# Two 64-row matmuls in the two halves of TensorE's array, in place of two zero-padded 128-row ones, for attention scores and the scan's masked products

## Chip, cores and metric

One core of one Trainium2 chip. The metric is the device time of one launch in microseconds (us), median of several runs. PE is TensorE's matmul, PEld its weight load, DVE VectorE, ACT ScalarE, POOL GpSimd, SP SyncE.

## What is computed

Two layers (`DEPTH`) of a hybrid network over 512 latent tokens and 128 context tokens. Each layer normalises and modulates its input, projects it once, and gives the columns to three mixers: a bidirectional RWKV-7 scan (4 heads of 64 features, width 256), differential attention (4 heads, each with **two maps of 64 features** and 128 value features), and a Hyena long convolution. Their outputs go through one output projection and then a squared-ReLU MLP. The two parts that matter here, from the reference:

```
s = jnp.einsum('bqhmd,bkhmd->bhmqk', qblk, k).astype(jnp.float32) * scale     # d = 64, m = 2 maps
p = jax.nn.softmax(s, axis=-1)
wts = p[:, :, 0] - lam * p[:, :, 1]
...
sa = jnp.einsum('bhvk,bhk->bhv', s, -kk_t)                                    # scan, 64 features per head
s = (s * w_t[:, :, None, :] + sa[..., None] * (kk_t * a_t)[:, :, None, :]
     + v_t[..., None] * k_t[:, :, None, :])
```

The kernel computes the scan in chunks of 128 tokens. For a chunk and a head it needs four 128x128 products over 64 features: (B or K) against (Z and R), each masked to its triangle.

## The kernel before

The five token tiles of 128 (four latent, one context) go through a layer in stages: input projection with Hyena and the operands of the scan, attention, scan, output projection, MLP. The instructions are written in Python order, but a scheduler that simulates the program (`schedule_with_timeline_sim=True`, L1772) sets the order on every engine; a pool's buffer that is still read holds an instruction back in that order.

**Attention** (L610 to L731) treats units of one head and one token tile: 4 heads x 5 tiles x 2 layers = 40 units. Three stages of successive units are issued interleaved.

- `at_head` (L637) loads a head's keys `kr` and queries. The queries stand in `qp` twice, a plane for each map, with the other map's 64 rows set to zero by two memsets on POOL (L645, L646), so that a product over 128 rows gives one map's scores. The rotated queries are written by two DVE additions of 64 rows each (L659).
- `at_scores` (L671): for each of two maps, scores of 128 queries against 640 keys (512 and 128 columns, L682 and L683; a context tile has 128 columns alone, L685) into a PSUM tile `pss` of two banks; the minimum (DVE, L687); the exponential with its sum (ACT, L689). Then DVE combines the two maps (L698). There are two `pss` buffers: map 0 takes one, map 1 the other.
- `at_values` (L701) transposes the weights (`pst`, L170) and multiplies by the values (`pso`, L714); `at_out` normalises and transposes back (`psy`).

**Scan** (`rw_begin`, `rw_scan`, `rw_inverse`, `rw_states`): 40 chunks (2 layers, 2 head pairs, 2 directions, 5 tiles), two by two in 20 groups. `rw_inverse` (L1001) first makes the masked products of each chunk. ACT copies B and K into a zeroed tile `bp`, one head's 64 rows at a time (L1019, L1020), the other head's rows staying zero; then for q = B, K and for each head e a 128-row matmul of 256 columns (L1025) into a PSUM bank `b` for each q, and a DVE product with the mask for each bank (L1026), giving `gb` and `gk`. POOL makes the fp16 matrix `m` from `gb` (L1032). Six doublings follow on PE (L1053, L1058, L1060), each with DVE and ACT steps between. `rw_states` then carries the states. Groups, states of both directions and the next modulation's products (`psmod`, L293) are woven together. The first four chunks' products are issued during the last units of attention.

Of the kernel before, what the change touches and what calls it, by code (L numbers as in the profile page):

```python
# [9 lines left out]
F32 = mybir.dt.float32  # L10
# [3 lines left out]
ALU = mybir.AluOpType  # L14
# [16 lines left out]
# columns of the small-vector table  # L31
# [15 lines left out]
def _consts():  # L47
    """Arrays that depend on the shapes alone."""
# [63 lines left out]
class Net:  # L112
# [26 lines left out]
    def split(self, h, l, src, he="v", le="v"):  # L139
        """h + l = src exactly to 24 bits, each of 12 bits."""  # L140
# [31 lines left out]
    def mm3(self, out, a, b, first, last):  # L172
        """out += a[0..1]^T b[0..1] over the split parts"""
# [23 lines left out]
    def setup(self):  # L197
# [15 lines left out]
        # conditioning: silu(c), silu(c_ctx) as columns padded to 32  # L213
# [24 lines left out]
    def small(self, l):  # L238
        """small vectors of layer l"""
# [12 lines left out]
        nlam = self.t(pl, [P, 1], F32, "nlam")       # -lambda  # L252
# [8 lines left out]
        hb = self.t(pl, [P, 8], F32, "hb")           # halves of w0, a0  # L261
# [48 lines left out]
    def mod_cols(self, rows):  # L310
        """the rows as columns: (q, 32 j + c), of which c < 2 used"""
# [20 lines left out]
    def mod_rows(self, rows, js):  # L332
        """gate * g_post of latents and context, into DRAM"""
# [5 lines left out]
    def mod_gate(self, d, pool):  # L339
        """the same on every partition"""  # L340
# [30 lines left out]
    def rstd(self, pool, ss, n, eps, shape, nm="rstd"):  # L371
        """(ss / n + eps) ** -0.5"""
# [32 lines left out]
    def denseB(self, pss, srcs, act, order=None, need=None):  # L405
        """token-major: 512 columns into 5 PSUM tiles [128, 512]; srcs: per pair of k tiles [128, 2, 512]"""
# [19 lines left out]
    def dense_apart(self, ws, act):  # L426
        """the same, one token tile after the other, with weights loaded before: yields (tile, PSUM)"""
# [8 lines left out]
    def ff_load(self, sa, px):  # L436
        """the weight side of a pair, in split parts: B11 B21, then T1 B22, T2 T3, T4"""
# [36 lines left out]
    def ff_plain(self, sa, sb, px, A, tmp, f):  # L474
        """two column tiles in eight products"""
# [41 lines left out]
    def ff_first(self, ys):  # L517
        """the blocks of the first half of the tokens"""
# [8 lines left out]
    def ff_rest(self, ys, A, pool, tmp):  # L527
        """the others: first those that plain products need"""
# [60 lines left out]
    def headscale(self, pool, sq, n, eps, fn):  # L589
        """sq: feature-major tile; (sum over a head / n + eps) ** -0.5, per head, back on its features: fn(slice, PSUM)"""  # L590
# [19 lines left out]
    def attention(self, l, pool, head, fill):  # L610
        """the stages of successive (head, token tile) units are issued interleaved"""
# [25 lines left out]
    def at_head(self, l, h):  # L637
        """q and k of a head, with their positions; k: latents, cache, context"""
# [5 lines left out]
        qp = self.at_tile("qp")  # L644
        nc.gpsimd.memset(qp[64:, 0], 0.0)  # L645
        nc.gpsimd.memset(qp[:64, 1], 0.0)  # L646
        for m in range(2):
            r = slice(64 * m, 64 * m + 64)
            nc.sync.dma_start(qp[r, m, TL:], self.Qd[h][r, TL:])
        for isq in range(2):  # L650
# [5 lines left out]
            if isq:  # L656
                for m in range(2):
                    r = slice(64 * m, 64 * m + 64)
                    nc.vector.tensor_tensor(out=qp[r, m, :TL], in0=u[r], in1=sh[r], op=ALU.add)  # L659
            else:  # L660
                nc.vector.tensor_tensor(out=kr[:, :TL], in0=u, in1=sh, op=ALU.add)
# [9 lines left out]
    def at_scores(self, u, pool):  # L671
        """both maps' exponentials (the products come with the factor -1/8), and their difference (times the first map's sum)"""
# [1103 lines left out]
```

## Time and profile before

| | |
|---|---|
| runs of the kernel before | 2267.98, 2269.1, 2275.34 us, median 2269.1 |
| the profiled execution: span, first to last instruction | 2272.8 us |
| mean granted TensorE clock | 0.968 |
| busy share PE, PEld, DVE, ACT, POOL | 94%, 80%, 64%, 36%, 35% |

The profiled execution's own device time is listed in no other form than its span, which lies 3.7 us (0.16%) above the median of the runs. Differences below are worked out on the span's rows and applied to the median.

Stages by the first and last instruction of their lines, in us from the span's start: attention 389 to 471 and 1474 to 1573 (the first part of the second lies beside the last products of the stage ahead), scan 471 to 700 and 1573 to 1762.

How to read it: a matmul of two fp32 operands is two instructions (passes) in the trace, so the 160 products of L1025 stand as x320. A record's duration has the pipeline's depth in it; the time that a matmul takes of PE is the distance between successive starts. The shapes show rows x columns of the weights (`64*128` is a matmul over 64 rows).

### The profile page before, as it was taken

The page shows a single profiled execution, that of the slowest core. Times are in us where ns is not written, and L with a number is a line of the kernel's source. Part 1 is how long each engine was busy: PE and PEld are TensorE (multiplying, and loading weights), DVE is VectorE, ACT ScalarE, POOL GpSimd, SP SyncE. Part 2 cuts the span into 40 slices and gives each one's busy share as a digit, 9 for nine tenths or more (in the row PEclk, how much of TensorE's full clock was granted, in tenths as well). Part 3 has the DMA queues.
Part 4 walks back from the last instruction along what each step waited for, and adds up shares of the span by engine and source line. Part 5 has one row for each costly group of instructions (what it writes and reads, how often), then busy time and mean ns, then how long its engine had stood idle before and what let it go on. Part 6 is the DMA issues. An engine that isn't in the chain of part 4 may idle for free.

```text
span 2272.8 us, 34001 instructions
## 1 busy us (share of the span) xinstructions
PE 2141.8 (94%) x13236; PEld 1815.5 (80%) x13236; DVE 1453.2 (64%) x2188; ACT 825.1 (36%) x1644; POOL 802.4 (35%) x781
## 2 busy tenths in 40 slices
PE   7999998899999899999999999989999989999998
PEld 2799985566687799898988999756588878989896
DVE  6776657865575764655666575886576484647475
ACT  4542232553342533222324323355344352313131
POOL 3433433641112424351522343363112232524251
PEclk8899998999999899999999999999999999999999
DMA  8244432135405222222244343222510512222233
GB/s 303 78 140 157 131 99 67 54 114 197 169 3 182 75 84 76 86 72 93 74 168 173 105 121 101 80 70 96 197 46 23 201 53 84 84 75 84 84 100 123
DMA packets 86070, 245.42 MB, mean 108 GB/s; under 512 B 12195, under 2 KB 24995, under 8 KB 85908
## 3 DMA queue, kind: packets, MB, share of 16 engines
q1 hardware_dynamic: 80148, 222.34, 28.8%
q0 software_dynamic: 5760, 20.91, 3.0%
q8 instruction: 104, 1.70, 0.3%
q14 instruction: 58, 0.48, 0.1%
HBM read 214.80 MB, written 28.87 MB: 107 GB/s over the span
## 4 chain that ended last, share of the span: by engine, by line
PE 43%; DVE 6%; issue 3%; POOL 3%; ACT 2%; DMA 2%; DVEq 0%; SPq 0%; POOLq 0%; ACTq 0%
PE psB L176 5%; PE psB L177 5%; PE psA L388 5%; PE psB L175 5%; PE psF L177 3%; PE psF L176 3%; PE psF L175 3%; PE b L1025 1%; PE psmod L293 1%; PE pss L682 1%; DMA ffb<-in_w_ff_dram 1%; PE pso L714 1%; PE psD L177 1%; PE psD L176 1%; PE psD L175 1%
## 5 line engine op out<-in xcount | busy, mean ns | idle before, releaser
L388 PE MATMUL psA<-act,wh 128*128 128x320 f32 x1472 | 305.6, 321 | 1.2 <-ACT uhr L1503 0.5
L388 PEld LDWEIGHTS psA<-act,wh 128*128 128x128 f32 x1472 | 241.0, 194 | 10.7 <-issue 8.0
L177 PE MATMUL psB<-wh,f 128*128 128x512 f32 x560 | 218.1, 389 | 0.0
L176 PE MATMUL psB<-wl,f 128*128 128x512 f32 x560 | 218.0, 389 | 0.0
L143 POOL TENSOR_TENSOR wl<-wr,wh 128x1024 fp32r<-128x1024 f32 x42 | 105.2, 2505 | 308.5 <-DVE wh L149 140.6
L175 PE MATMUL psB<-wh,f 128*128 128x512 f32 x560 | 209.1, 389 | 0.0
L388 PE MATMUL psA<-act,wl 128*128 128x320 f32 x736 | 183.0, 319 | 0.8 <-DVE wl L143 0.8
L143 DVE TENSOR_TENSOR wl<-wr,wh 128x1024 fp32r<-128x1024 f32 x84 | 106.6, 1269 | 64.4 <-ACT wh L147 62.8
L457 POOL TENSOR_TENSOR fft<-ffb 128x512 f32<-128x512 f32 x56 | 90.9, 1623 | 127.2 <-DVE wl L143 53.8
L388 PEld LDWEIGHTS psA<-act,wl 128*128 128x128 f32 x736 | 128.8, 194 | 4.6 <-issue 3.1
L147 ACT CAST wh<-wr 128x1024 fp32r<-128x1024 f32 x63 | 66.1, 1050 | 168.4 <-PE psB L177 82.5
L177 PEld LDWEIGHTS psB<-wh,f 128*128 128x128 f32 x560 | 105.1, 188 | 21.9
L175 PEld LDWEIGHTS psB<-wh,f 128*128 128x128 f32 x560 | 105.1, 188 | 21.7
L176 PEld LDWEIGHTS psB<-wl,f 128*128 128x128 f32 x560 | 105.1, 188 | 21.6
L149 DVE CAST wh<-wr 128x1024 fp32r<-128x1024 f32 x63 | 49.9, 793 | 93.5 <-PE psB L177 64.8
L1054 DVE TENSOR_TENSOR x<-b,cmask 128x512 f16<-128x512 f32 x120 | 80.4, 685 | 33.0 <-PE b L1053 32.7
L147 ACT CAST f<-ffr 128x640 fp32r<-128x640 f32 x64 | 43.8, 726 | 154.1 <-DVE ffr L497 154.1
L1063 ACT CAST t<-px 128x512 f16<-128x512 f32 x100 | 58.7, 588 | 101.4 <-PE px L1058 100.3
L505 DVE TENSOR_TENSOR ffr<-ffr,psF 128x320 f32<-128x320 f32 x140 | 67.3, 481 | 37.3 <-POOL ffr L505 20.3
L505 POOL TENSOR_TENSOR ffr<-ffr 128x320 f32<-128x320 f32 x56 | 55.3, 987 | 94.6 <-DVE ffr L505 86.6
L1025 PE MATMUL b<-ZR,bp 128*128 128x256 f32 x320 | 85.4, 392 | 1.5 <-ACT awt L147 0.7
L177 PE MATMUL psF<-ffS,wl 128*128 128x320 f32 x256 | 80.3, 314 | 5.0 <-DVE wl L143 5.0
(461 smaller groups left out, 6041.7 us busy)
## 6 DMA issues: line engine op xcount, KB each, us to landing
wr<-in_w_mod_dram SPq DMA_DIRECT2D x83, 512.0 KB
wr<-in_w_ff_dram SPq DMA_DIRECT2D x72, 512.0 KB
wr<-in_w_in_dram SPq DMA_DIRECT2D x46, 512.0 KB
x<-x SPq DMA_DIRECT2D x30, 512.0 KB
ffa<-in_w_ff_dram SPq DMA_DIRECT2D x28, 512.0 KB
ffb<-in_w_ff_dram SPq DMA_DIRECT2D x28, 512.0 KB
dft<-in_k_dftf_dram POOLq DMA_DIRECT2D x16, 512.0 KB, 7.2
dft<-in_k_dfti_dram POOLq DMA_DIRECT2D x16, 512.0 KB, 4.7
```

Source lines behind the costliest of these rows:

```text
L143: eng.tensor_tensor(out=l, in0=src, in1=h.bitcast(F32), op=ALU.subtract)
L147: self.nc.scalar.copy(out, in_)
L149: self.nc.vector.tensor_copy(out, in_)
L175: nc.tensor.matmul(out, a[0], b[0], start=first, stop=False)
L176: nc.tensor.matmul(out, a[0], b[1], start=False, stop=False)
L177: nc.tensor.matmul(out, a[1], b[0], start=False, stop=last)
L388: self.nc.tensor.matmul(ps[:, hf, :320], (h, l)[a][:, k * P:(k + 1) * P], act[b][k][:, hf * 320:hf * 320 + 320], start=k == 0 and i == 0, ...
L457: sub = lambda o, x, y: nc.gpsimd.tensor_tensor(out=o, in0=x, in1=y, op=ALU.subtract)
L505: add = lambda o, a, b, e=nc.vector, op=ALU.add: e.tensor_tensor(out=o, in0=a, in1=b, op=op)
L1025: nc.tensor.matmul(ps[:, 2 * e:2 * e + 2], bp[:, q, e], s["ZR"][:, :, j], start=True, stop=True)
L1054: nc.vector.tensor_tensor(out=vw(x16), in0=vw(ps), in1=cm(i), op=ALU.mult)
L1063: nc.scalar.copy(t16, ps1)
```

## The change

`at_head` no longer makes two padded planes: `qp` is one plane, both maps' features stacked on 128 rows, one load and one DVE addition, no memset. `at_scores` takes both `pss` buffers at once and multiplies rows 0 to 63 for map 0 and rows 64 to 127 for map 1, written in turn. In the scan the `bp` tiles, their memsets and the ACT copies go; each head's product reads its 64 rows of `BK` and `ZR` directly. The products are now stored by chunk (`gt[i]`, with q, head and mask inside) instead of by q, and a PSUM bank now belongs to a head e instead of to q. POOL's operation for `m16` becomes two, one per chunk.

```
 # at_head
-        qp = self.at_tile("qp")
-        nc.gpsimd.memset(qp[64:, 0], 0.0)
-        nc.gpsimd.memset(qp[:64, 1], 0.0)
-        for m in range(2):
-            r = slice(64 * m, 64 * m + 64)
-            nc.sync.dma_start(qp[r, m, TL:], self.Qd[h][r, TL:])
+        qp = self.at_tile("qp")[:, 0]
+        nc.sync.dma_start(qp[:, TL:], self.Qd[h][:, TL:])
...
-            if isq:
-                for m in range(2):
-                    r = slice(64 * m, 64 * m + 64)
-                    nc.vector.tensor_tensor(out=qp[r, m, :TL], in0=u[r], in1=sh[r], op=ALU.add)
-            else:
-                nc.vector.tensor_tensor(out=kr[:, :TL], in0=u, in1=sh, op=ALU.add)
+            nc.vector.tensor_tensor(out=(qp if isq else kr)[:, :TL], in0=u, in1=sh, op=ALU.add)
 # at_scores
+        pss = [self.t(self.pss, [P, 1024], F32, "pss") for _ in range(2)]
+        for a, b, o in ((0, TL, 0), (TL, T, TL)) if lat else ((T, T + TC, 0),):
+            for m in range(2):
+                r = slice(64 * m, 64 * m + 64)
+                nc.tensor.matmul(pss[m][:, o:o + b - a], H["qp"][r, j * P:(j + 1) * P], H["kr"][r, a:b],
+                                 start=True, stop=True)
         for m in range(2):
-            q = H["qp"][:, m, j * P:(j + 1) * P]
-            ps = self.t(self.pss, [P, 1024], F32, "pss")
-            if lat:
-                nc.tensor.matmul(ps[:, :TL], q, H["kr"][:, :TL], start=True, stop=True)
-                nc.tensor.matmul(ps[:, TL:T], q, H["kr"][:, TL:T], start=True, stop=True)
-            else:
-                nc.tensor.matmul(ps[:, :TC], q, H["kr"][:, T:T + TC], start=True, stop=True)
+            ps = pss[m]
 # rw_inverse
-            bp = self.bp[self.nbp % 2]          # (B | K) by head, the other head's rows zero
-            self.nbp += 1
-            nc.scalar.copy(bp[:64, :, 0], s["BK"][:64, :, j])
-            nc.scalar.copy(bp[64:, :, 1], s["BK"][64:, :, j])
-            gm = self.gmask[:, s["d"]].rearrange("p (a t) -> p a t", a=2).unsqueeze(1).to_broadcast([P, 2, 2, P])
-            for q, g in ((0, gb), (1, gk)):
-                ps = self.bank4(self.b1, "b1")
+            gm = self.gmask[:, s["d"]].unsqueeze(1).to_broadcast([P, 2, 2 * P])
+            ps = [self.bank4(self.b1, "b1") for _ in range(2)]
+            for q in range(2):
                 for e in range(2):
-                    nc.tensor.matmul(ps[:, 2 * e:2 * e + 2], bp[:, q, e], s["ZR"][:, :, j], start=True, stop=True)
-                nc.vector.tensor_tensor(out=g[:, i].rearrange("p e a t -> p e (a t)"),
-                                        in0=ps.rearrange("p (e a) t -> p e (a t)", e=2),
-                                        in1=gm.rearrange("p e a t -> p e (a t)"), op=ALU.mult)
+                    hs = slice(64 * e, 64 * e + 64)
+                    nc.tensor.matmul(ps[e][:, 2 * q:2 * q + 2], s["BK"][hs, q, j], s["ZR"][hs, :, j],
+                                     start=True, stop=True)
+            for e in range(2):
+                nc.vector.tensor_tensor(out=gt[i][:, :, e].rearrange("p q a t -> p q (a t)"),
+                                        in0=ps[e].rearrange("p (q a) t -> p q (a t)", q=2), in1=gm, op=ALU.mult)
             yield
```

The scheduler orders the changed program anew. Two places, both on PE, show how.

First place: PE, attention of the first layer, second head, token tiles 1 and 2. `pss_927` and `pss_930` (before), `pss_927` and `pss_928` (now) are the two maps of tile 1; `pst`, `psy` and `pso` are transposes and value products of other units. Before:

```order
L682 MATMUL pss_927_4067<-kr_839_3847,qp_840_3850 128x512
L683 MATMUL pss_927_4067<-kr_839_3847,qp_840_3850 128x128
L170 MATMUL pst_918_4048<-ident_25_130,pexp_888_3977 128x128
L682 MATMUL pss_930_4074<-kr_839_3847,qp_840_3850 128x512
L683 MATMUL pss_930_4074<-kr_839_3847,qp_840_3850 128x128
L714 MATMUL pso_919_4051<-vt_812_3781,awt_917_4047 128x128
L682 MATMUL pss_953_4142<-kr_839_3847,qp_840_3850 128x512
L683 MATMUL pss_953_4142<-kr_839_3847,qp_840_3850 128x128
```

Now:

```order
L674 MATMUL pss_927_4059<-kr_839_3843,qp_840_3846 128x512
L674 MATMUL pss_927_4059<-kr_839_3843,qp_840_3846 128x128
L170 MATMUL psy_904_4010<-ident_25_130,aon_900_4002 128x128
L674 MATMUL pss_928_4060<-kr_839_3843,qp_840_3846 128x512
L674 MATMUL pss_928_4060<-kr_839_3843,qp_840_3846 128x128
L706 MATMUL pso_919_4043<-vt_812_3777,awt_917_4039 128x128
L674 MATMUL pss_953_4130<-kr_839_3843,qp_840_3846 128x512
L674 MATMUL pss_953_4130<-kr_839_3843,qp_840_3846 128x128
```

Map 0's two matmuls still come first and map 1's two behind them, with a 128-row transpose between; what the program text writes in turn does not stand in turn.

Second place: PE, the end of the first layer's attention, where the first scan chunk's products come in. `b1_1164` and `b1_1165` (before) are the banks of B and K, `b1_1162` and `b1_1163` (now) those of the two heads. Before:

```order
L682 MATMUL pss_1167_4677<-kr_1053_4389,qp_1054_4392 128x512
L683 MATMUL pss_1167_4677<-kr_1053_4389,qp_1054_4392 128x128
L714 MATMUL pso_1153_4640<-vt_1119_4563,awt_1150_4630 128x128 x4
L1025 MATMUL b1_1164_4668<-ZR_677_2884,bp0_1160_4660 128x256 x2
L714 MATMUL pso_1153_4640<-vt_1119_4563,awt_1150_4630 128x128
L1025 MATMUL b1_1165_4672<-ZR_677_2884,bp0_1160_4660 128x256 x2
L682 MATMUL pss_1170_4684<-kr_1053_4389,qp_1054_4392 128x512
```

Now:

```order
L674 MATMUL pss_1165_4655<-kr_1053_4377,qp_1054_4380 128x512
L674 MATMUL pss_1165_4655<-kr_1053_4377,qp_1054_4380 128x128
L706 MATMUL pso_1153_4624<-vt_1119_4547,awt_1150_4614 128x128 x4
L1012 MATMUL b1_1162_4646<-ZR_677_2884,BK_681_2900 128x256 x2
L706 MATMUL pso_1153_4624<-vt_1119_4547,awt_1150_4614 128x128
L1012 MATMUL b1_1163_4647<-ZR_677_2884,BK_681_2900 128x256 x2
L674 MATMUL pss_1166_4656<-kr_1053_4377,qp_1054_4380 128x512
```

Head 0's two products (q = B, K) stand together, then a 128-row value product, then head 1's two: in place of one switch of bank there is now one of array rows.

## Rows read from the trace of the kernel before

**Rows 1.** Busy time of the engines in six stretches, attention (two per layer) and scan; columns first.

```profile
core 0: us, PE busy (x) PEld busy (x) DVE busy (x) ACT busy (x) POOL busy (x), PEclk, DMA share, GB/s
388.00:430.00 42.00, 31.50 (x142) 21.74 (x141) 36.04 (x68) 20.44 (x62) 26.06 (x36) 0.89 0.32 99
430.00:471.00 41.00, 38.50 (x224) 28.08 (x223) 30.17 (x63) 28.08 (x96) 20.86 (x44) 0.99 0.10 32
471.00:700.00 229.00, 220.95 (x1859) 159.69 (x1858) 140.25 (x271) 93.69 (x212) 45.36 (x55) 0.99 0.40 131
1478.00:1530.00 52.00, 42.18 (x211) 29.09 (x210) 44.45 (x90) 28.40 (x93) 33.73 (x54) 0.90 0.21 64
1530.00:1573.00 43.00, 38.94 (x228) 29.36 (x227) 30.53 (x58) 27.44 (x92) 19.92 (x40) 1.00 0.11 38
1573.00:1762.00 189.00, 183.26 (x1680) 139.06 (x1679) 120.06 (x237) 81.04 (x175) 39.44 (x41) 1.00 0.31 103
```

**Rows 2.** Chain that ended last, by line, in the second layer's scan (1573 to 1762).

```profile
by line: PE b L1025 15.3%; PE psmod L293 15.0%; PE px L1058 7.3%; PE px L1060 6.8%; PE b L1053 6.8%; PE px L1073 5.7%; PE pq L1099 4.7%; PE px L1068 4.3%; PE pq L1093 4.0%; PE pq L1129 3.4%; PE pq L1104 2.4%; PE pq L1090 2.4%; PE pq L1105 2
```

**Rows 3.** The same in the second layer's attention (1478 to 1573).

```profile
by line: PE pss L682 22.4%; PE pso L714 14.8%; ACT pexp L689 7.9%; issue 5.9%; PE pss L683 5.1%; PE pst L170 5.1%; PE b L1025 4.1%; DVE amin L687 3.5%; DVE pexp L698 2.9%; DVE acf L694 2.6%; DVE ql L655 2.4%; POOL aon L728 2.4%; ACT awt L14
```

**Rows 4.** What PE waited for longest, in the second layer's scan.

```profile
PE ps L917 <- DVE yacc L1132: 1.6, 1, 1.6
```

**Rows 5.** The same in the second layer's attention.

```profile
PE pss L682 <- ACT pexp L689: 5.4, 7, 2.6
```

**Rows 6.** PE around a 64-row product in the stage of the scan's operands: start, length, line, count.

```profile
1392.73 0.60 PE L388 MATMUL psA<-act,wh 128*128 128x320 f32 x3
1393.17 0.38 PE L170 MATMUL pshb<-ident,ksq 128*128 128x128 f32 x2
1393.48 1.34 PE L585 MATMUL ps<-u,w 64*128 64x320 f32 x4
1393.85 0.70 PE L585 MATMUL ps<-u,w 64*128 64x320 f32 x2
1394.12 0.70 PE L585 MATMUL ps<-u,w 64*128 64x320 f32 x2
1394.75 0.56 PE L388 MATMUL psA<-act,wl 128*128 128x320 f32 x2
1395.15 0.31 PE L388 MATMUL psA<-act,wh 128*128 128x320 f32 x1
```

**Rows 7.** PE at products in separate column groups: modulation (32 columns), then outputs (64 columns).

```profile
1617.16 1.91 PE L293 MATMUL psmod<-wr,sc 128*32 128x512 f32 x12
1619.00 0.40 PE L1058 MATMUL px<-x,tt 128*128 128x128 f16 x4
...
1710.51 0.45 PE L1129 MATMUL pq<-gk,vt 128*64 128x128 f32 x4
1710.78 0.40 PE L1130 MATMUL pq<-gb,sA 128*64 128x128 f32 x4
1711.11 0.48 PE L1025 MATMUL b<-ZR,bp 128*128 128x256 f32 x1
```

**Rows 8.** ACT and PE in attention: the sums that end two exponentials, then the next unit's scores.

```profile
1489.62 0.20 ACT L689 ACTIVATION_READ_ACCUMULATOR pexp<-pss,amin 128x1 f32 x1
...
1489.87 1.13 PE L682 MATMUL pss<-kr,qp 128*128 128x512 f32 x2 [1.14 <-ACT pexp L689]
...
1490.39 0.21 ACT L689 ACTIVATION_READ_ACCUMULATOR pexp<-pss,amin 128x1 f32 x1
...
1491.06 1.28 PE L714 MATMUL pso<-vt,awt 128*128 128x128 f32 x10
```

**Rows 9.** Groups of instructions by line and shape that the change removes or halves.

```profile
L1025 PE MATMUL b<-ZR,bp 128*128 128x256 f32 x320 | 85.4, 392 | 1.5 <-ACT awt L147 0.7 <-DVE x L1054 0.6
L1019 ACT COPY bp<-BK 64x256 f32<-64x256 f32 x40 | 16.0, 401 | 24.2 <-PE b L1025 19.1 <-POOL bp L845 4.9
L659 DVE TENSOR_TENSOR qp<-ql,rsh 64x512 f32<-64x512 f32 x16 | 10.9, 683 | 0.1
```

More of the change, by code (lines that the diff above doesn't have):

```diff
@@ L842, in rw_begin @@
         nc = self.nc
-        self.bp = [self.t(pool, [P, 2, 2, P], F32, f"bp{i}", bufs=1) for i in range(2)]
-        for x in self.bp:
-            nc.gpsimd.memset(x, 0.0)
-        self.nbp = self.ng = 0
+        self.ng = 0
         def groups(p):
@@ L1013, in rw_inverse @@
         self.ng += 1
-        gb, gk = (x.rearrange("p (i e a t) -> p i e a t", i=2, e=2, a=2) for x in (gb, gk))
-        G["gb"], G["gk"] = gb, gk
+        gt = [x.rearrange("p (q e a t) -> p q e a t", q=2, e=2, a=2) for x in (gb, gk)]
+        G["g"] = gt
         for i, (s, j) in enumerate(ent):
-            bp = self.bp[self.nbp % 2]
-            self.nbp += 1
-            nc.scalar.copy(bp[:64, :, 0], s["BK"][:64, :, j])
-            nc.scalar.copy(bp[64:, :, 1], s["BK"][64:, :, j])
-            gm = self.gmask[:, s["d"]].rearrange("p (a t) -> p a t", a=2).unsqueeze(1).to_broadcast([P, 2, 2, P])
-            for q, g in ((0, gb), (1, gk)):
-                ps = self.bank4(self.b1, "b1")
-                for e in range(2):
-                    nc.tensor.matmul(ps[:, 2 * e:2 * e + 2], bp[:, q, e], s["ZR"][:, :, j], start=True, stop=True)
-                nc.vector.tensor_tensor(out=g[:, i].rearrange("p e a t -> p e (a t)"),
-                                        in0=ps.rearrange("p (e a) t -> p e (a t)", e=2),
-                                        in1=gm.rearrange("p e a t -> p e (a t)"), op=ALU.mult)
+            gm = self.gmask[:, s["d"]].unsqueeze(1).to_broadcast([P, 2, 2 * P])
+            ps = [self.bank4(self.b1, "b1") for _ in range(2)]
+            for q in range(2):
+                for e in range(2):
+                    hs = slice(64 * e, 64 * e + 64)
[4 more added lines that the diff above has]
+                                        in0=ps[e].rearrange("p (q a) t -> p q (a t)", q=2), in1=gm, op=ALU.mult)
             yield
@@ L1031, in rw_inverse @@
         m16 = H("m16", 5)
-        nc.gpsimd.tensor_tensor(out=m16.rearrange("p (i e) t -> p i e t", i=2), in0=gb[:, :, :, 0],
-                                in1=self.ident.unsqueeze(1).unsqueeze(1).to_broadcast([P, 2, 2, P]), op=ALU.add)
+        for i in range(2):
+            nc.gpsimd.tensor_tensor(out=m16[:, 2 * i:2 * i + 2], in0=gt[i][:, 0, :, 0],
+                                    in1=self.ident.unsqueeze(1).to_broadcast([P, 2, P]), op=ALU.add)
         if mixed:
@@ L1067, in rw_inverse @@
         for u in us:
-            nc.tensor.matmul(ps[:, u], gb[:, u // 2, u % 2, 0], t16[:, u], start=True, stop=True)
+            nc.tensor.matmul(ps[:, u], gt[u // 2][:, 0, u % 2, 0], t16[:, u], start=True, stop=True)
         nc.vector.tensor_tensor(out=t16, in0=ps, in1=t16, op=ALU.subtract)
@@ L1080, in rw_states @@
         nc, O = self.nc, self.O
-        gb, gk, tf = G["gb"], G["gk"], G["tf"]
+        gt, tf = G["g"], G["tf"]
         for i in idx:
@@ L1092, in rw_states @@
                 es = slice(64 * e, 64 * e + 64)
-                nc.tensor.matmul(px[:, es], gk[:, i, e, 0], vt[:, j, es], start=not lat, stop=e == 1 or not lat)
+                nc.tensor.matmul(px[:, es], gt[i][:, 1, e, 0], vt[:, j, es], start=not lat, stop=e == 1 or not lat)
             X = self.t(pool, [P, P], F32, "sX")
@@ L1128, in rw_states @@
                 es = slice(64 * e, 64 * e + 64)
-                nc.tensor.matmul(py[es], vt[:, j, es], gk[:, i, e, 1], start=not lat, stop=False)
-                nc.tensor.matmul(py[es], SA[:, es], gb[:, i, e, 1], start=False, stop=True)
+                nc.tensor.matmul(py[es], vt[:, j, es], gt[i][:, 1, e, 1], start=not lat, stop=False)
+                nc.tensor.matmul(py[es], SA[:, es], gt[i][:, 0, e, 1], start=False, stop=True)
             if j in done:
```

## Prediction

> **What bounds the kernel now.** I read the stages first, because the change touches only attention and scan. The stretches [rows 1] show two kinds of stage. In the scan PE is busy 221 of 229 us and 183 of 189 us, at a clock of 0.99 and 1.00, while ACT and DVE stand at 41% to 64%; in the first half of each attention PE has 31.5 of 42 us and 42.2 of 52 us, and DVE more than PE (36.0 and 44.5 us); in the second half PE leads again (38.5 of 41, 38.9 of 43). The chain of the second scan [rows 2] is PE nearly throughout, L1025 and the modulation first with 15% each. The chain of attention [rows 3] is mixed: scores 22% and 5%, value products 15%, but exponentials, minima, combinations and POOL between them. The waits agree: in the scan PE's longest is 1.6 us [rows 4], in attention it waits seven times, 5.4 us, for an exponential to free a score buffer [rows 5]. So in the scan each microsecond on PE is a microsecond of time; in attention about half of one is.
>
> **What a matmul costs.** Successive passes of 320 fp32 columns start 0.27 us apart (1393.85, 1394.12 [rows 6]), so 128 columns take 0.107, 256 take 0.21, 512 take 0.43. These are the passes of a 64-row product: half the rows alone makes nothing shorter. The gain can only come from two halves running beside each other.
>
> Do parts of the array run beside each other? The trace has it for column groups: twelve modulation passes of 512 columns take from 1617.16 to 1619.00, 1.84 us, where one after the other would be 12 x 0.43 = 5.1; eight passes of L1129 and L1130 take from 1710.51 to 1711.11, 0.60 us with the return to the whole array in it, where singly they are 0.86 [rows 7]. The program has L1129 and L1130 of one half ahead of those of the other, so the halves overlap even when four passes stand between. Row halves I take to do the same if nothing else stands between; no row here shows it.
>
> **What a change of shape costs.** The array must go over to the other shape and back. Between the start of L170 at 1393.17 and that of the L388 at 1395.15 lie 1.98 us [rows 6]. The passes in it are 2 x 0.107, 4 x 0.27 and 2 x 0.147 (L388 starts three times in 0.44 us before), 1.58 us. The rest, 0.40, is one way out and one back: **0.20 us per change of shape**, in which neither a matmul streams nor a weight load hides.
>
> The Trainium skill, "TensorEngine Tiling (Array Packing)", gives up to twice the speed for a contraction of at most 64 (section Theoretical Speedup). By that alone, every pair at half its time, the scan's 40 chunks would save 34 us of PE and the 32 latent units 34, half of it on the path: 51 us, 2218. The same page says that changing the tiling mode drains TensorE (section Key Properties), without a price; by the 0.20 us above, the drains as they stand in the new order would take back about as much (250 x 0.20). Which of the two wins hangs on the order, next.
>
> **The change, part by part.**
>
> (1) *Do the halves meet?* The order of PE's instructions decides it, and the two places shown with the change are typical. Counted over the program, the two maps of a latent unit stand together in 14 of 32 units; in 18 something of 128 rows is between. In the scan the two heads of a chunk stand together in 2 of 40 chunks; 76 bursts of two products stand alone. A buffer for the second half comes free later than for the first, and the scheduler fills the time with other work.
>
> (2) *Scan, loss.* Over both scans the order now holds 338 changes of array shape where it held 212 (the modulation's and the outputs' column groups), 126 more: 126 x 0.20 = **+25 us**. (3) *Scan, gain.* Two chunks overlap; a chunk is 8 passes of 0.21, 1.7 us, half of it saved: **-1.7**. PE's short waits there, 1.6 us the longest [rows 4], take back perhaps 4 in both scans. Scan: **+19**.
>
> (4) *Attention, loss.* No change of shape before, 124 now (61 and 63): +25 us of PE. In the first halves of the stage PE has 10 us per layer without any record [rows 1], and many bursts begin after a wait, where the array is empty anyway. (5) *Attention, gain.* A latent map is 2 x 0.43 + 2 x 0.107 = 1.07 us, which is the most that a pair can save. But map 1's buffer is not free when map 0 starts: at 1489.87 map 0 starts as the exponential of the unit before ends (1489.62 + 0.20), and the other exponential ends at 1490.60 [rows 8], 0.73 us later. That leaves 0.34 us of overlap; I take 0.4 for 14 units, with up to 1.07 where both are free: -6.5. So +18 us of PE; half of it on the path, **+9**.
>
> (6) *Work taken off.* The 80 ACT copies of L1019 and L1020 (0.40 each, 32 us), 8 of the 16 DVE additions of L659 (0.68 each, 5.5 us) [rows 9], the POOL memsets and 8 small loads on SP's queue. ACT is 41% to 43% busy in the scan, so its 32 us are worth nothing there; what hides them is PE's own work, and without it they would return at most the 19 us for which ACT stood before a copy waiting for L1025 [rows 9]. DVE leads in the first half of attention: 6 of the 8 additions saved (heads 1 to 3 of both layers) lie in the stage, 4 us, worth **-1**. Fewer loads on SP move nothing, since no row shows PE waiting for a query.
>
> (7) *A wait added.* `m` on POOL needed only the bank of B; it now needs both heads' banks, so it waits for one more pair of matmuls and one more mask product (0.43 us, and some 0.68 like the DVE addition of 512 columns [rows 9], an estimate) in 20 groups, while its second half is half as long. The groups are woven eight deep and PE has other matmuls to do: 0, at most 20 x 1.1 = 22 us if nothing covered it, at least nothing. POOL's queue behind it is short (45 of 229 us busy [rows 1]). `gt[0]` is freed earlier than `gb` was: 0. Elsewhere the scheduler moves a few matmuls of the output projection and of the MLP's beginning: 0, some 3 us either way.
>
> **Sum.** +19 + 9 - 1 = +27 us. On the profiled execution 2272.8 + 27 = 2299.8; its span is 3.7 us above the median, so on the median **2269.1 + 27 = 2296 us**, 1.2% slower. A measurement of this kernel can tell about 0.3%, 7 us, from no change.
>
> **Rivals.**
>
> *The halves meet after all* (faster). Place: the 40 chunks and 32 latent units. If TensorE took the second half up beside the first across what stands between, or the order on the chip let them meet, a chunk would give 0.85 - 0.40 and a unit 1.07 - 0.40: 40 x 0.45 = 18 and 32 x 0.67 = 21, half of it on the path, 29 us: 2240. In the scan it decides from the point where 0.85 per pair outweighs the 25 us of changes, 30 of 40 pairs. For it: column halves overlap over four passes [rows 7]. Against: what stands between here uses all 128 rows, and the way back from 64 rows costs an empty array [rows 6]. Chance 0.10.
>
> "TensorE: Matmul & The Clock Gate", section Why this matters for your kernels, of the Trainium skill, says that small-row matmuls at distinct row groups run concurrently. By that rule, with every pair met, the rival's 2240 would come; no run here shows it for rows.
>
> *The change costs nothing to speak of* (same). The changes of shape fall into waits and the copies' relief pays for the rest: attention 0, scan +25 - 1.7 - 19 = +4, 2273. For it: PE's busy share has the pipeline's depth in it, so some of the "busy" 97% is slack; ACT did wait 19 us at L1019. Against: PE's waits for others in the scan are small [rows 4]. Chance 0.17.
>
> *Everything on the path* (slower still). Attention is PE bound in its second halves; a contiguous pair makes PE stand at map 1's buffer with the transposes and value products queued behind. 250 changes x 0.20 - 1.7 = +48: 2317. For it: before, PE filled the time until map 1's buffer was free with value products (1491.06 [rows 8]). Against: PE's free 10 us per layer in the first halves [rows 1]. Chance 0.20.
>
> The forecast itself has 0.53.
>
> **How the numbers follow.** Faster by over 0.3% (under 2262): the first rival and a little of the second, 0.12. Within 0.3%: most of the second and the lower edge of the forecast, 0.16. Slower: 0.72. The range leaves out the first rival (0.10) and what lies beyond the third (0.08): 2262 to 2320. The likeliest case's own range is 2279 to 2312: the price of a change between 0.15 and 0.25 us moves the sum of (2) and half of (4) by 9 either way, (7) and the moved matmuls add up to 8.
>
> **What would show it.** L1012 passes with a start distance of 0.21 us, alone in their half, an empty 0.1 us and a bare weight load on either side; scan stretches longer by some 10 us per layer with PE as busy as before; 14 pairs of score matmuls partly overlapped; ACT some 32 us less busy. The forecast is wrong if the starts of the two heads' products lie within a few hundredths of a microsecond in most chunks, if the change of shape around L1012 and L674 costs clearly less than 0.20 us, or if the scan is not longer.

## Result and the profile after

The changed kernel takes **2303.9 us** (median of 4 runs, 2302.0 to 2313.8) against 2270.9 us (4 runs, 2268.0 to 2275.3): ratio 1.0158, interval 1.0131 to 1.0184. Forecast were 2296 us in a range of 2262 to 2320. The profiled spans differ by 27.1 us (2299.9 to 2272.8), less than the 33 us between the medians: the span of the kernel before is longer than three of its four runs, that of the changed kernel belongs to the shortest of its four. It is by chance that 27.1 is so near the forecast's +27.

First the stretches of the changed kernel in one profile, read from its own stage limits (first score product, last value product, last product of the scan); columns as in [rows 1]. (By these limits the first layer's attention of the kernel before ends at 491, not at 471; its last 20 us stand in [rows 1] under the scan.)

```profile
389.00:431.00 42.00, 35.78 (x140) 22.72 (x137) 33.71 (x66) 18.49 (x59) 21.43 (x31) 0.71 0.28 86
431.00:497.00 66.00, 62.02 (x322) 43.12 (x320) 41.30 (x84) 36.60 (x123) 28.76 (x60) 0.95 0.12 39
497.00:709.00 212.00, 205.19 (x1736) 139.20 (x1735) 121.60 (x240) 67.99 (x142) 37.08 (x47) 1.00 0.39 130
1484.00:1536.00 52.00, 42.93 (x183) 28.36 (x181) 38.24 (x74) 23.54 (x75) 24.33 (x35) 0.77 0.26 82
1536.00:1593.00 57.00, 52.27 (x281) 35.98 (x280) 37.56 (x77) 31.92 (x109) 27.89 (x56) 1.00 0.13 40
1593.00:1786.00 193.00, 188.88 (x1667) 135.91 (x1667) 118.61 (x230) 67.64 (x141) 37.86 (x45) 1.00 0.29 95
```

Two things stand here. The scans are PE throughout, as in [rows 1], and longer. And in the first part of each attention the granted clock is 0.71 and 0.77, where it was 0.89 and 0.90: nothing in the prediction spoke of that. ACT has lost its 80 copies: it is busy for 794.5 us with 1564 instructions, instead of 825.1 us with 1644.

Waits and chain answer to [rows 4, 5] and [rows 2]. The changed kernel's longest waits of PE, in the second scan and then in the second attention:

```profile
PE pq L1093 <- DVE so L1109: 0.9, 1, 0.9
...
PE pss L674 <- ACT pexp L681: 8.8, 8, 2.9
```

Its chain by line, second scan:

```profile
by line: PE b L1012 17.0%; PE psmod L293 14.7%; PE px L1047 7.6%; PE b L1042 6.7%; PE px L1049 6.2%; PE px L1062 5.5%; PE pq L1088 4.2%; PE px L1057 4.1%; PE pq L1082 3.7%; PE pq L1118 3.3%; DMA wr<-in_w_mod_dram 2.6%; PE pq L1093 2.5%; PE 
```

PE's waits in the scan are as short as before, and the masked products have gone from 15.3% to 17.0% of the chain: the scan's loss sits on PE, not in a new wait.

All kernels of this study, from one profile each: length in us of attention (first score product to last value product) and scan (to its last product) in both layers, all by starts, and the granted clock in the first 60 us of each attention. e1 to e12 are the experiments of the next section.

| kernel | attention 1 | scan 1 | attention 2 | scan 2 | clock | ratio to before, interval |
|---|---|---|---|---|---|---|
| before | 102.5 | 201.6 | 100.8 | 184.8 | 0.91, 0.91 | 1 |
| changed | 108.2 | 212.1 | 108.4 | 192.9 | 0.74, 0.80 | 1.0158 (1.0131 to 1.0184) |
| e1 attention alone | 109.3 | 202.6 | 120.3 | 186.2 | 0.74, 0.69 | 1.0087 (1.0068 to 1.0107) |
| e2 scan alone | 98.7 | 211.6 | 98.2 | 192.8 | 0.97, 0.97 | 1.0069 (1.0051 to 1.0087) |
| e12 as e2, on 128 rows | 96.3 | 206.1 | 95.3 | 187.5 | 0.97, 1.00 | 0.9987 (0.9973 to 1.0001) |
| e3 whole change, on 128 rows | 93.9 | 205.9 | 96.7 | 186.1 | 1.00, 0.94 | 0.9976 (0.9963 to 0.9989) |
| e4 as e2, heads met | 103.3 | 193.4 | 104.1 | 179.2 | 0.94, 0.94 | 0.9955 (0.9937 to 0.9973) |
| e5 whole change, all met | 104.3 | 193.7 | 107.0 | 179.8 | 0.86, 0.77 | 0.9994 (0.9980 to 1.0008) |
| e6 as e4, padded scores together | 103.1 | 194.8 | 100.2 | 180.2 | 0.97, 0.97 | 0.9944 (0.9924 to 0.9963) |
| e7 as e6, another bank for the doublings | 103.6 | 199.3 | 96.5 | 182.8 | 0.97, 1.00 | 0.9983 (0.9965 to 1.0001) |
| e11 as e6, without the late waits | 99.8 | 193.1 | 99.2 | 179.0 | 0.97, 0.97 | 0.9933 (0.9916 to 0.9950) |
| e8 attention alone, 64 rows in heads 2 and 3 | 102.5 | 202.1 | 103.3 | 184.9 | 0.94, 0.97 | 1.0005 (0.9990 to 1.0019) |
| e9 changed, with added transposes | 107.7 | 210.3 | 115.2 | 192.7 | 0.89, 0.77 | 1.0178 (1.0155 to 1.0201) |
| e10 before, with added transposes | 103.0 | 203.1 | 103.9 | 184.6 | 0.97, 0.94 | 1.0029 (1.0013 to 1.0045) |

The stages between differ from those of the kernel before by -7 to +4 us in kernels that do not touch them, so stage lengths of single profiles are to be read with that in mind. The attention of the row "before" is itself a long sample: e2 and e12 have the same code there, and up to the tenth unit's value copy they take 54.1 and 53.6, 54.0 and 53.0 us at a clock of 0.97 to 1.00, where it takes 58.4 and 56.5 at 0.91.

### The profile page after: what moved, and what is told of

It is laid out like the page before. It is cut to its first block, busy times and chain, and to the rows that moved or that the text cites. A ratio compares the mean times of both kernels' runs of the same rounds, so it can differ in the third digit from the quotient of the medians.

```text
span 2299.9 us, 33871 instructions
## 1 busy us (share of the span) xinstructions
PE 2173.4 (95%) x13236; PEld 1811.7 (79%) x13236; DVE 1448.8 (63%) x2180; ACT 794.5 (35%) x1564; POOL 789.2 (34%) x781
## 4 chain that ended last, share of the span: by engine, by line
PE 42%; DVE 7%; issue 3%; POOL 3%; DMA 2%; ACT 2%; SPq 0%; DVEq 0%; POOLq 0%; ACTq 0%
PE psB L176 5%; PE psB L177 5%; PE psB L175 5%; PE psA L388 5%; PE psF L177 3%; PE psF L176 3%; PE psF L175 2%; PE b L1012 2%; PE psmod L293 1%; PE pss L674 1%; PE pso L706 1%; DMA ffb<-in_w_ff_dram 1%; DVE ffr L497 1%; PE px L1047 1%; PE psD L175 1%
## 5 line engine op out<-in xcount | busy, mean ns | idle before, releaser
L674 PE MATMUL pss<-kr,qp 64*128 64x128 f32 (+1 forms) x288 | 92.2, 495 | 15.9 <-ACT pexp L681 15.9
L674 PEld LDWEIGHTS pss<-kr,qp 64*128 64x128 f32 x288 | 47.9, 209 | 59.2 <-issue 32.6
L1012 PE MATMUL b<-ZR,BK 64*128 64x256 f32 x320 | 88.0, 402 | 0.7 <-ACT awt L147 0.7
```

Of the source, the lines that this page charges most:

```text
L674: nc.tensor.matmul(pss[m][:, o:o + b - a], H["qp"][r, j * P:(j + 1) * P], H["kr"][r, a:b], start=True, stop=True)
L1012: nc.tensor.matmul(ps[e][:, 2 * q:2 * q + 2], s["BK"][hs, q, j], s["ZR"][hs, :, j], start=True, stop=True)
```

## Experiments

**One part alone (e1, e2).** The functions that each kernel has in the changed form:

```
e1: +at_head +at_scores
e2: +rw_begin +rw_inverse +rw_states
```

> Attention of the change, scan of the kernel before. Theory (each burst of 64-row matmuls that stands alone costs two changes of array shape): attention keeps 112 of its 124 changes of shape, so nearly all of the 13 us by which the two attention stages grew stays, and the scans are as before: 2271 + 12 = 2283 us, ratio 1.005. If the two halves of the change do not add (one of them pays for the other), this run and the next do not sum to the change's +33 us between the medians: under 2275, or over 2295.

> Scan of the change, attention of the kernel before. Theory: 124 changes of shape more in the two scans and 16 at the end of attention, less 2 us of overlap: the 18 us by which the scans grew, 2271 + 19 = 2290 us, ratio 1.008. A rival that puts the loss on attention alone expects under 2278.

Measured: 2290.3 us and 2286.8 us against 2270.6. The parts add (0.87% + 0.69% = 1.56%, the whole 1.58%). The scan's came as expected; attention alone costs 20 us, not 12, and both its stages begin at a low clock.

**All rows at once (e3).** The changed structure, but no change of shape:

```
-                r = slice(64 * m, 64 * m + 64)
+                r = slice(None)
...
-                    hs = slice(64 * e, 64 * e + 64)
+                    hs = slice(None)
```

> The changed kernel with its buffers, banks, waits and order of storage, but every product takes all 128 rows, so that no change of shape is left in attention and 212 in the scans, as before. It leaves out the separation of the maps and heads: a score and a masked product sum over the features of both. Theory (the shape costs the time): the whole loss goes, and about 11 us of overlap with it; attention and scans return to the lengths of the kernel before or a little less, since ACT's 80 copies stay out: 2262 to 2272 us, ratio 0.996 to 1.001. Rival (both score buffers taken at once, a bank for each head, POOL waiting for both banks): the loss stays, 2290 us or more, ratio over 1.008. In between: both have a part.

Measured: 2266.7 us. The whole loss goes, and the clock in attention stays at 1.00 and 0.94. Buffers, banks and waits of the new structure, taken together, are not what costs. The second edit alone, in e2 (e12):

> The kernel with the changed scan alone, but its masked products take all 128 rows; every instruction stands in the same order on PE as with 64 rows, so the difference of the two is the price of 140 changes of shape alone (less 2 us of overlap), and the difference to the kernel before is that of the new structure (a bank for each head, no ACT copies). It leaves out the separation of the heads: each masked product sums over both heads' features. With the scan on 64 rows the time was 2287 us, 16 us over the kernel before. Theory as predicted (0.20 us per change): 2287 - 28 + 2 = 2261 us. Theory after the run on 128 rows throughout (0.12 us per change there, and some 4 us of loss by the structure): 2287 - 17 + 2 = 2272 us, ratio 1.0005. Rival (the structure's waits hold most of the loss): 2280 us or more.

Measured: 2270.4 us, 16.4 us less than e2, with PE's instructions in the same order; by the two ratios to the kernel before (e2 and e12 were measured on different chips) it is 18.6. Adding back the 1.7 us of overlap that I had worked out for the two chunks that meet, 18 to 20 us for 140 changes: 0.13 to 0.145 us per change, by the intervals some 0.04 more or less, and not 0.20. Since all 13236 passes stand in the same order, the two traces can be laid beside each other burst by burst. The 76 bursts of four 64-row passes take 16.5 us longer than the same bursts on 128 rows, 0.234 us each in the median; the two chunks that meet (eight passes) take 0.62 us less each. Of the 152 borders of these 76 bursts 16 touch column groups, where the shape changes anyway; 16.5 us over the other 136 is **0.12 us per change**. One of the bursts, PE in the second scan of e2:

```profile
1668.10 0.39 PE L1057 MATMUL px<-tt,x 128*128 128x128 f16 x4
1668.42 1.13 PE L1020 MATMUL b<-ZR,BK 64*128 64x256 f32 x4
1669.48 0.40 PE L1055 MATMUL px<-x,tt 128*128 128x128 f16 x4
```

The same place in e12:

```profile
1663.43 0.39 PE L1057 MATMUL px<-tt,x 128*128 128x128 f16 x4
1663.66 1.08 PE L1020 MATMUL b<-ZR,BK 128*128 128x256 f32 x4
1664.58 0.39 PE L1055 MATMUL px<-x,tt 128*128 128x128 f16 x4
```

From the start of L1057 to that of L1055 it is 1.38 us with 64 rows and 1.15 with 128: 0.23 us for the way out and back, 0.115 each.

**The heads met (e4).** In e2, the first product of a chunk waits for the last reader of the second bank too (`old` is the b1 tile allocated last; a dependency is added from that product to the last instruction that reads it):

```
+            old = self.last["b1"]
             ps = [self.bank4(self.b1, "b1") for _ in range(2)]
...
+                    if q == e == 0:
+                        self.both(mm.ins, old)
```

> Scan of the change, attention of the kernel before, and the first product of a chunk waits for the last reader of the second bank as well, so that both banks are free when it starts: in the order on PE 38 of 40 chunks now have their four products in turn, head 0, head 1, head 0, head 1. Theory (row halves run beside each other, the order kept them apart): 38 x 0.85 us of overlap, 63 changes of shape more than before at 0.20: -32 + 13 = -19, and some 4 us for the longer wait: 2256 us, ratio 0.993 (range 2248 to 2266). Rival A (row halves gain little even side by side): no overlap, the changes stay: 2284 us or more, ratio 1.006. Rival B (the wait for both banks costs what the overlap gains): 2271 us, ratio 1.000, with PE idle longer before these products.

Measured: 2261.7 us, ratio 0.9955, inside the expected range: faster than the kernel before. Rivals A and B both fall. A met chunk on PE:

```profile
1607.90 0.33 PE L1104 MATMUL pq<-vt,gk 128*128 128x64 f32 x2
1608.17 1.13 PE L1032 MATMUL b<-ZR,BK 64*128 64x256 f32 x8
1609.23 0.43 PE L1104 MATMUL pq<-vt,gk 128*128 128x64 f32 x2
```

Eight passes take 1.06 us from start to the next start, as long as four did above; the trace's single records have the second head's pass start 0.007 us after the first's, four times over. In both scans the time in which PE streams columns (a pass counted by its columns, what runs side by side once) falls from some 308 to 277 us. Of these 31 us the masked products make 27: 32 of the 38 met chunks lie in the scans, 32 x 0.85. The rest is the modulation's products in column groups, of which more run beside each other in the new order. The gaps between passes grow from some 79 to 96 us: 43 of the 63 changes lie here, 5 us at 0.12, and PE's time without any record grows from 8 to 18 us. None of its waits of over 0.15 us stands right before a masked product, so what the wait for both banks costs is not seen directly. The scans are 14 us shorter.

**The maps met too (e5).** The same dependencies in the whole change; in attention `old` is the `pss` tile allocated last, its reader the exponential that frees the second buffer:

```
+                if a in (0, T) and m == 0 and old:
+                    self.both(mm.ins, old)
```

> The change whole, with the halves made to meet in attention too: the first product of a unit also waits for the exponential that frees the second score buffer, as in the scan for the second bank. In the order all 40 units and 34 of 40 chunks and more have their halves in turn. The scans should be as in the run before with the heads met, 14 us shorter than in the kernel before. For attention, theory A (the clock): with scores on 64 rows the granted clock in the first part of the stage falls again (0.71 and 0.77 in the change, 1.00 and 0.93 with 128 rows in the same structure), so that 34 us of overlap buy nothing: attention as long as in the kernel before or up to 8 us longer per layer, 2257 to 2272 us. Rival B (overlap counts, the clock does not follow the rows): clock 0.9 or more, each attention 8 us or more shorter than before: 2240 us or less.

Measured: 2270.2 us, inside theory A's range. The scans give 12.8 us; attention with all its units met is 8 us longer than before, both layers together. The clock is 0.86 and 0.77 in the first 60 us. So in attention the full overlap buys nothing, as theory A says; but the clock, its reason, is only a part of it. From the tenth unit's value copy to the seventeenth's the clock is 1.00, and there too the met kernel takes 32.2 us where the kernel before takes 30.9:

```profile
446.12:478.35 32.23, 25.25 (x165) 17.78 (x167) 21.38 (x41) 19.54 (x69) 15.37 (x32) 1.00 0.10 33
```

PE is busy for 25.3 us there instead of 29.4, and its waits of over 0.15 us have grown from 1.5 to 7.4 us: 2.2 for the normalised outputs (`psy`), 2.0 for a score buffer, the others for weights and their copies. With the maps met, PE waits for the other engines at full clock as well. A run with the maps met and the clock kept up was not made.

**Padded scores, heads met (e6).** The scan of e4 and `at_head` of the kernel before; `at_scores` takes both buffers at once as in the change, with all 128 rows:

```
-                nc.tensor.matmul(pss[m][:, o:o + b - a], H["qp"][r, j * P:(j + 1) * P], H["kr"][r, a:b],
+                nc.tensor.matmul(pss[m][:, o:o + b - a], H["qp"][:, m, j * P:(j + 1) * P], H["kr"][:, a:b],
```

> Scan with the heads met; attention with the zero-padded 128-row queries of the kernel before, but both score buffers taken at once and the products written in turn, as in the change. Theory: the structure is worth what the run on 128 rows showed (attention 8.6 and 4.1 us shorter than before), less the padding's memsets and half additions: 2262 - 10 = 2252 us, ratio 0.992 (range 2245 to 2259), granted clock of the first parts of attention 0.92 or more. Rival (that gain came from the padding's work left out, not from the structure): attention as before, 2260 us.

Measured: 2258.9 us, the clock as expected, and the time at the border between both: against e4's 2261.7 the intervals overlap, and attention is 103.1 and 100.2 us, as before. The rival holds as far as the structure goes: from the first score product to the tenth unit's value copy e6 takes 55.4 and 54.8 us, no less than e2 and e12 with the code of the kernel before (53.0 to 54.1). That the padding's work left out is what e3 gained is not shown. e3 takes 51.1 and 53.9 us there, at a clock of 1.00 and 0.94: in both layers together 5 us less than e6 and 2 less than e12. Of the 10 us by which e3 is shorter than the kernel before (58.4 and 56.5), e12 has 8 with padded scores.

**Another bank for the doublings (e7).** In e6, for the doublings' first product (L1053 before):

```
-            ps = self.bank4(self.b1, "b1")
+            ps = self.bank4(self.px, "px")
```

> As the kernel of the run before this one, but the six doublings' first product takes a bank of the other three (px) instead of one of the two banks that the masked products use. Theory (the waits for the second bank, which that product holds, cost the met scan some 14 us): PE's gaps in the scans shrink, up to 8 us less than the run before. Rival (three banks for the doublings become the wait): as long or longer, with PE waiting at the doublings.

Measured: 2265.9 us, 7 us slower than e6, scans 199.3 and 182.8 us: the theory falls, and the rival's time holds. Its reason is not shown: PE's waits of over 0.15 us at the doublings (L1064 and L1069 of e7) are 1.1 and 1.6 us in the two scans, 0.7 and 0.9 in e6.

**The late waits left out (e11).** In e6, the chunks that are issued beside attention do not wait for the second bank (`met` is set where `rw_scan` starts the weave):

```
-                    if q == e == 0:
+                    if q == e == 0 and self.met:
```

> Padded 128-row attention with both score buffers taken at once and the scan's heads met, as in the run of that name, but the first eight chunks, whose products are issued beside the last units of attention, do not wait for the second bank; the other 32 do. Theory (there the wait holds up attention's value products: units 17 to 20 take some 4 us per layer longer than in the kernel before): 2259 - 6 = 2253 us, range 2247 to 2259. Rival (single bursts there cost as much as the wait): 2259 us.

Measured: 2255.7 us, ratio 0.9933: inside the range, though its interval overlaps e6's, so the median alone does not tell the two apart. The trace does: the last three units take 12.9 us in both layers (18.2 and 15.6 in e6, 13.8 before). It has the lowest ratio here, 0.7% under the kernel before and, by the two ratios, 2.2% under the changed one.

**Shape or clock (e8).** The attention of the change with padded queries, the scan of the kernel before. Heads 0 and 1 padded, heads 2 and 3 in halves:

```
+                q, r = H["qp"][:, m], slice(None)
+                if u["h"] > 1:
+                    r = slice(64 * m, 64 * m + 64)
```

> Attention alone: heads 0 and 1 with zero-padded 128-row products, heads 2 and 3 in 64-row halves, both score buffers taken at once; scan of the kernel before. It tells the price of the shape from the price of the clock. Theory (two costs: the low clock in the first ten units, the changes of shape, some 0.6 us per unit, in the last ten): the first ten units take some 35 us per layer as on 128 rows (41 in the change), with a granted clock of 0.92 or more; units 10 to 16 take 35 us (31 on 128 rows, 35 in the change). Time 2271 - 14 + 10 = 2267 us, range 2260 to 2275. Rival (the clock falls wherever 64-row products run): it is under 0.9 in the second half and the time over 2280.

Measured: 2274.7 us, ratio 1.0005 (0.9990 to 1.0019), at the range's edge. The clock is 0.94 and 0.97 in the first 60 us and 1.00 in both layers over units 11 to 17, so it does not fall wherever 64-row products run: the rival is out. From the first unit's copy to the tenth's it is 42.5 and 35.4 us (35 expected; the first layer missed that), for units 11 to 17 32.6 and 34.4 us (35 expected; 31 on 128 rows). The early heads gained less than I expected: from the first score product to the tenth unit's value copy they take 55.3 and 55.8 us, as padded scores do in the other kernels, and it was e3's 51.1 and 53.9 that I had reckoned with.

**More work, if it lifts the clock.** The transposes of heads 0 and 1 made three times, in the changed kernel (e9) and in the kernel before (e10):

```
-            for i in range(w_ // P):
+            for i in list(range(w_ // P)) * (3 if u["h"] < 2 else 1):
```

> The changed kernel with the transposes of the weights in heads 0 and 1 made three times over into the same place: 84 passes of 128 rows and 128 columns more per layer, 84 x 0.107 = 9.0 us of PE per layer at the full clock, twice that at the low one. Theory (in the first ten units the change loses time to the granted clock, which fell to 0.71 and 0.77 there): with more 128-row work between the scores the clock is 0.85 or more, and the first ten units (60.4 and 60.6 us from the first score product to the tenth unit's values) take no more than 62 us although they hold 9 us more of work; 2304 us, at most 2310. Rival (the low clock has nothing to do with the work on PE): the clock stays near 0.7, the added passes cost 9 to 18 us per layer: 2320 us or more.

> The kernel before with the same added transposes, as a control: 9.0 us more of PE per layer in the first ten units (58.5 and 56.5 us, clock 0.88 and 0.90). Theory: a part of the 10 us per layer in which PE has nothing takes them up, and the clock, already near full, has little to give back: 2 to 6 us longer per layer, 2276 to 2284 us. If fillers cost nothing here as well, the run on the changed kernel says nothing on the clock.

Measured: e9 2311.2 us, between the two expectations; e10 2279.0 us, as expected. e9's two layers differ. The first 60 us of its attentions:

```profile
388.00:448.00 60.00, 55.66 (x306) 40.63 (x305) 42.58 (x86) 28.76 (x90) 27.18 (x44) 0.89 0.23 73
1491.00:1551.00 60.00, 51.42 (x251) 37.69 (x250) 39.51 (x77) 24.03 (x75) 22.83 (x35) 0.77 0.23 72
```

In the first layer the clock rose from 0.74 to 0.89 and 9.0 us of added passes cost nothing (attention 107.7 us instead of 108.2); in the second it stayed low (0.80, now 0.77) and they cost 6.8 us (115.2 instead of 108.4). So the clock is worth about what the added work is, but adding work does not lift it reliably. This run is inconclusive on what sets the clock.

## Why the prediction was right, and where it was not

The sign, the chief mechanism (the order keeps the halves apart, each lone burst pays two changes of shape) and the total hold: +27 us forecast, +33 between the medians. But it came out so near partly by luck: the price of a change of shape was too high by 0.08 us, some 15 us of the sum (10 in the scan, 5 in attention), and a loss of a like size was missing, in the first ten units of each attention, where the granted clock is low.

**(1) held.** Overlap appears where the order lets the halves meet, and only there; e4 and e5 show that it needed nothing but the order.

**(2) was mis-sized.** 0.20 us per change of shape is 0.12 (e2 against e12), and "clearly less than 0.20" was one of the signs of being wrong that the forecast named. The step that failed is reading all 0.40 us beside the passes in [rows 6] as change of shape: a burst on 128 rows has part of it too, as e12's 0.92 us for four passes of 0.21 shows. That is 0.08 of it; what the rest is, no run takes apart. (The three lines of L585 in [rows 6] show the same four passes, from the first, the second and the third on.) So 126 changes cost 15 us, not 25. That the scans still came out 18 us longer (10.5 and 8.1), as the term said, hides a second loss: with the new structure on 128 rows (e12) the scans are 7 us longer than before, with as many passes in them. There the whole is unchanged, because attention is 12 us shorter: 4 of them in the last three units of the two layers (11.7 us each instead of 13.8), a stretch that held some of ACT's copies, 8 in the first ten units, where the clock is 0.97 and 1.00 instead of 0.91.

**(3) held**: 1.7 us of overlap in the scans of the changed kernel. The 4 us of waits that it subtracted are not to be seen.

**(4) lacked a cost.** "Half of it on the path" was for changes of shape alone. From the tenth unit's value copy to the seventeenth's, where the clock is 1.00, the changed kernel takes 35.3 us in both layers, e3 31.4: 3.9 us for 31 changes, 0.126 each, all of it on the path. Next to nothing overlaps there. In the first ten units it is 60.4 and 60.6 us against e3's 51.1 and 53.9, for 29 and 31 changes, which by 0.13 are 4 us. The other 5 and 3 us come with the clock. 5 us of overlap per layer bought nothing there either; how much of that went to the clock and how much to waits, as in e5, no run takes apart. Attention's first passes show the clock. In the changed kernel:

```profile
397.70 2.50 PE L674 MATMUL pss<-kr,qp 64*128 64x512 f32 x4 [0.31 <-ACT pexp L681]
400.13 1.33 PE L170 MATMUL pst<-ident,pexp 128*128 128x128 f32 x5
```

In e3, at the same place of the program:

```profile
397.72 1.35 PE L674 MATMUL pss<-kr,qp 128*128 128x512 f32 x4 [0.70 <-ACT pexp L681]
398.90 0.71 PE L170 MATMUL pst<-ident,pexp 128*128 128x128 f32 x5
```

Scores and transposes both take nearly twice as long (2.43 us from start to start instead of 1.18). The granted clock of these six microseconds and of the six before, in the changed kernel:

```profile
390.00:396.00 6.00, 4.06 (x15) 2.19 (x16) 6.00 (x15) 2.92 (x7) 3.92 (x4) 1.00 0.82 247
396.00:402.00 6.00, 5.15 (x13) 2.62 (x11) 6.00 (x12) 1.39 (x4) 3.20 (x5) 0.54 0.35 106
```

And in e3:

```profile
390.00:396.00 6.00, 4.64 (x19) 2.52 (x18) 5.78 (x14) 2.92 (x7) 3.51 (x4) 1.00 0.82 240
396.00:402.00 6.00, 4.16 (x17) 2.23 (x15) 6.00 (x12) 2.42 (x6) 2.86 (x5) 1.00 0.26 86
```

Inside the second of these stretches, at 396.5, the changed kernel's clock goes from its full level (2.4 GHz, 1.00) to its lower one (1.2 GHz, 0.50); before it fell, PE had run 64-row scores and been busy 4.1 of 6 us (4.6 in e3, on 128 rows). Up to there PE runs the same products in both. The clock falls on 128 rows too, but for less long: in the first attention it is at the lower level for 13.7 and 17.1 us in the changed kernel, three times for 3.4 us in the kernel before, not at all in e3.

**(5)** was too low: 10 us of overlap in attention, not 6.5, all of it in the first ten units of the two layers.

**(6) and (7)** come to nothing together, as said: e12, without the copies on ACT and with POOL waiting for both heads, is at 0.9987. Apart they are not measured, and part of the 7 us by which e12's scans are longer may be the wait of (7). The padding's work, put at -1, is worth 2 to 5 us for both layers together (e3 against e12 and e6 above).

So the sum: by 0.12 the 250 changes are 30 us, the overlap takes back 12, the structure without padding 4 (e3). That is 14 of 33 us. The other 19 lie in attention's first ten units, by what they show: 5 and 3 us beyond their changes, which come with the clock, and 10 of overlap that bought nothing there. That the clock could make so much is an estimate from its means: 0.963 over the changed kernel's runs against 0.972 over e3's is 21 us of full-clock time on PE, an upper bound for what it cost. The forecast had no clock in it and a price two thirds too high.

**Rivals.** *The halves meet* was put at 2240 us: made to meet, they give 2262 in the scan alone and 2270 with attention. Its scan term was right in kind (-18 forecast, -14 measured), its attention term was wrong in sign. *No cost* did not come. *All on the path* was half right: its 2317 lies 13 us above the result, the forecast 8 below; where PE is at full clock attention's changes were on the path, but what it lost beside them was mostly the clock; PE's wait for a score buffer grew by 3.4 us in the second attention (5.4 in [rows 5], 8.8 above).

## What to carry to other kernels

Packing two half-height products pays only if they stand next to each other in the engine's order: give the first the wait of the second, and look at the order before counting on it. And it pays only where that engine is what the time waits for: the scans gained 14 us by it, attention nothing. Price a change of array shape by the same burst with and without it, not by what is left over around one. Ask what a change does to the granted clock in stretches where PE already waits often, and compare that column of the profile first.

## What the runs showed of the hardware

- Row halves of the array run beside each other: in a met chunk the second half's pass starts 0.007 us after the first's, and eight passes take as long as four. A change of shape between 128 and 64 rows costs 0.12 us (0.234 us for the way out and back, median of 76 bursts in e2 against e12).
- With scores on 64 rows in heads 0 and 1, the granted clock of attention's first 60 us was 0.69 to 0.89 in all four such kernels (changed, e1, e5, e9) and both layers; with 128 rows there it was 0.91 to 1.00 in the ten others. The mean over the whole program, listed for every run, says the same: 0.957 to 0.967 in the 26 runs of those four, 0.966 to 0.976 in those of the kernel before beside the experiments. e3 has the changed structure and waits, so the rows set it apart; how they do it, no run here tells. It is not for want of work on PE alone: in the second attention of e1 the clock stayed at the lower level for 34 us in which PE was busy for 33 (columns as in [rows 1]).

```profile
1510.97:1545.10 34.13, 32.94 (x98) 21.93 (x100) 14.57 (x30) 13.39 (x46) 9.97 (x23) 0.50 0.09 28
```

- In the later heads 64 rows do not bring the clock down: over units 11 to 17 it is 1.00 in the changed kernel, e1, e5, e8 and e9.
